# Moving the token operands of an encoder layer's matmuls by 64 to 192 bytes within SBUF

## The chip, the cores and the metric

The kernel runs on one core of a Trainium2 chip. The metric is the device time of one execution in microseconds; times before are the median of three timed runs, and one further execution was recorded by the hardware profiler. The core's engines are TensorE (matmuls, PE in the profile, with its weight loads as PEld), VectorE (DVE), ScalarE (ACT), GpSimd (POOL) and SyncE (SP), which here only issues transfers. SBUF is the memory that matmul operands are read from: 128 partitions, and an address is a byte offset within each of them. PSUM takes the matmuls' results.

## The reference

One layer of an encoder on 512 tokens of width 1024, with 256 memory tokens, all in float32:

```python
n = rms_norm(h, mix_norm_g)
proj = n @ w_in                                  # 1024 x 4608 columns
ya = s5_branch(proj[..., :OFF_U], ...)           # two scans and a GLU
yb = sgu_branch(zu, zv, ...)                     # gating within chunks of 128 tokens
h = h + (gate_a * (ya @ w_proj_a) + gate_b * (yb @ w_proj_b)) @ w_out
h = h + memory_cross_attention(rms_norm(h, g), memn, w_q, w_k, w_v, w_xo)   # 4 heads of 256
h = h + (silu(f @ w_gate) * (f @ w_up)) @ w_down # f = rms_norm(h, ffn_norm_g), width 2816
return rms_norm(h, final_norm_g)
```

`memn` is the normalised memory; keys and values come from it.

## The kernel before

**Split operands.** Every large matrix product is made of three matmuls in a rounded float32 format (`F32R`). Each operand is split into a high part (`hi`, a rounding copy on ScalarE) and a low part (`lo`, the difference, on VectorE; both in `split`, lines 85 and 86). A product is then hi·hi + hi·lo + lo·hi, three matmuls one after the other into one PSUM place (`mm3`, line 314; line 1264 for the FFN).

**Stationary and streamed.** A matmul holds 128 x 128 numbers of one operand in the array and streams the other through it. The stationary operand is loaded by an instruction of its own before each matmul. In `feat` and `product` the weights are stationary and the tokens are streamed, 512 or 256 of them; in `tokm` and the down product the tokens are stationary and 512 columns of weights are streamed. In the profile a matmul is written `out<-streamed,stationary`.

**Order.** A list `plan` has all weight blocks in order of use. Blocks of 512 KB are loaded some places ahead by SyncE's queue, split two ahead, and used. Nothing in this order depends on addresses. The stages are: the input projection with the scan woven in, the gates and merge, `w_out`, then keys (`w_k`, `feat` with 256 tokens), values (`w_v`, `tokm`), queries and attention per head, `w_xo`, the FFN's gate and up products, and the down product.

**The FFN.** The gate and up products use a Winograd-like scheme: a unit (512 columns of `w_gate` or `w_up`) takes seven products `1, 5, 2, 6, 3, 7, 4` of 24 matmuls with 256 tokens each, over sums of weight blocks and sums of token blocks. There are ten units, so 1680 matmuls of 256 columns at line 1264. Products 1, 2, 7 and 4 stream quarters of `fn`, the normalised tokens; products 5, 6 and 3 stream token sums made by `make_op` into tiles `s1`, `s2` and `s4` (`s` in the profile). A remainder of 256 columns is done by `gate_part` (`w_gate`: half of the tokens at a time, so 256 columns, with weights in `s` tiles: `pf<-fn,s`) and by `feat` (`w_up`: 512 columns, `pf<-fn,whi` and `pf<-fn,wlo`).

**Where operands lie.** Weight tiles `whi` and `wlo` take turns in six places whose byte offsets all have the remainder 320 modulo 512. Most token tiles (`xn`, `yb`, `mg`, `hn`, `mn`, the first `qq`) have the same remainder, so their distance from the weights is 0 modulo 512; two small pad tiles (`align`) see to that. Slices within the tiles are multiples of 512 bytes, so one remainder holds for the whole tile. Some tiles stand off on purpose: `token_slot(name, shift)` makes a tile that is 128 elements longer than its content and puts the content `shift` elements (4 bytes each) in; `fn` has shift 16, 64 bytes. `sums_place(i, k, n, shift)` does the same for the `s` tiles: `make_op` uses shift 80, 320 bytes, while weights and the down product's tokens in the same tiles use 0. The keys `kt_hi` and `kt_lo` stand 64 bytes off (tile `shift`). Distances before, streamed minus stationary, modulo 512:

| matmuls | streamed, stationary | columns | distance |
|---|---|---|---|
| most `feat` and `tokm` | tokens and weights, either way | 512 | 0 |
| keys, 192 | `mn`, `whi`/`wlo` | 256 | 0 |
| values, 96 | `whi`/`wlo`, `mn` | 512 | 0 |
| queries of the first head, 96 | `hn`, `whi`/`wlo` | 256 | 0 |
| scores | `kt`, `qq` | 256 | 64 |
| gate remainder, 96 | `fn`, `s` | 256 | 64 |
| up remainder, 48 | `fn`, `whi`/`wlo` | 512 | 64 |
| FFN products 1, 2, 7, 4 | `fn`, `whi`/`wlo` | 256 | 64 |
| FFN products 5, 6, 3 | `s`, `whi`/`wlo` | 256 | 320 |

The tag `mq` of the attention pool has two buffers: first `mn_hi` and `mn_lo`, 8192 bytes a partition each, later `qq` (one head's queries, both parts), the heads in turn.

Of the kernel before, what the change touches and what calls it, by code (L numbers as in the profile page):

```python
# [10 lines left out]
F32R = mybir.dt.float32r  # L11
# [6 lines left out]
P = 128  # L18
D = 1024
T = 512  # L20
NT = T // P
KD = D // P
M = 256
# [29 lines left out]
def hybrid_layer_kernel(  # L53
# [26 lines left out]
    def aux(name, shape=(P, 512)):  # L80
        return pa.tile(list(shape), F32, tag="aux", name=name)

    def split(dst_hi, dst_lo, src, lo_eng=None):

        nc.scalar.copy(dst_hi, src)  # L85
        (lo_eng or nc.vector).tensor_tensor(dst_lo, src, dst_hi.bitcast(F32), ALU.subtract)  # L86
# [23 lines left out]
    def sums_place(i, k, n, shift=0):  # L110
        t = sums_pool[0].tile([P, 2 * k * n + 128], F32R, tag=f"s{i}", name=f"s{i}", bufs=1)
        return t[:, shift:shift + 2 * k * n].rearrange("p (h k n) -> p h k n", h=2, k=k)
# [309 lines left out]
    def gain(src, name):  # L422
        t = np_.tile([P, D], F32, tag="gain", name=name, bufs=2)
        nc.sync.dma_start(t, src.partition_broadcast(P))
        return t
# [52 lines left out]
    def slot(tag, shape, dt, name):  # L478
        return sp.tile(list(shape), dt, tag=tag, name=name)

    def token_slot(name, shift=0):

        t = sp.tile([P, 2 * KD * T + 128], F32R, tag="B", name=name)
        hl = t[:, shift:shift + 2 * KD * T].rearrange("p (h k t) -> p h k t", h=2, k=KD)
        return hl[:, 0], hl[:, 1]
# [557 lines left out]
    ap_ = at.enter_context(tc.tile_pool(name="attn", bufs=1))  # L1043

    h = slot("A", (P, NT, D), F32, "h")
# [2 lines left out]
    hn_hi, hn_lo = token_slot("hn")  # L1048
    hn = (hn_hi, hn_lo)

    mn_hi = ap_.tile([P, KD, M], F32R, tag="mq", name="mn_hi", bufs=2)
    mn_lo = ap_.tile([P, KD, M], F32R, tag="mq", name="mn_lo", bufs=2)
    g_mem = gain(mem_norm_g, "g_mem")

    def mem_norm(t):
# [60 lines left out]

    def q_evac(m, j, ps):
        if j == 0:
            qq = ap_.tile([P, 2, 2, T], F32R, tag="mq", name="qq", bufs=2)
            qs[m // 2] = (qq[:, 0], qq[:, 1])  # L1120
        q_hi, q_lo = qs[m // 2]
        split(q_hi[:, j, :], q_lo[:, j, :], ps)
# [46 lines left out]
    for hd in range(XH):  # L1169
        feat(w_q, hd * XD, hn, KD, q_evac, parts=2 if hd == 0 else 1)  # L1170
        probs = scores(hd)
        if hd > 0:
            values(hd - 1, *pts.pop(0))
        later(1, lambda hd=hd, probs=probs: pts.append(turn_probs(hd, probs)))

    g_f = gain(ffn_norm_g[0], "g_f")
    ot = (ot_hi, ot_lo)
    fn_hi, fn_lo = token_slot("fn", 16)
    fn = (fn_hi, fn_lo)

    tokm(w_xo, 0, ot, KD, add_evac(0, 1, None), hook=lambda: values(XH - 1, *pts.pop()))
# [50 lines left out]
    a11, a12, a21, a22 = full[:, K0, T0], full[:, K1, T0], full[:, K0, T1], full[:, K1, T1]  # L1232

    def make_op(q, i, src):
        hl = sums_place(i, 4, 256, 80)
        ops[q] = (hl[:, 0], hl[:, 1])
        split(*ops[q], src)

    def sum1():
        V.tensor_tensor(a22, a21, a22, ALU.subtract)  # L1240
        make_op(5, 1, a22)

    def sum2():
        V.tensor_tensor(s3, a11, a21, ALU.subtract)
        V.tensor_tensor(a11, a22, a11, ALU.subtract)
        make_op(6, 2, a11)

    def sum4():
        V.tensor_tensor(a12, a12, a11, ALU.add)
        make_op(3, 4, a12)  # L1250
# [232 lines left out]
    for i in range(2):  # L1483
        p = aux("pcut", (P, 256))
# [37 lines left out]
```

## Time and profile before

| | us |
|---|---|
| median of three timed runs (918.16, 923.18, 923.67) | 923.18 |
| profiled execution | 915.85 |
| its span, first to last instruction | 914.1 |
| TensorE busy | 897.4 |
| weight loads busy | 789.2 |
| VectorE busy | 609.0 |
| ScalarE busy | 458.7 |
| mean granted TensorE clock | 0.994 |

The profile's times are of the one profiled execution, in microseconds from its first instruction. A busy TensorE is not one at its peak: matmuls are pipelined, the recorded duration of one is longer than the time until the next one starts, and only runs of many matmuls tell how quickly they follow each other. The chain of work that ended last is followed back from the last instruction; where TensorE never waits, it lists unbroken runs of matmuls with length and count.

### The profile page before, as it was taken

The page shows a single profiled execution, that of the slowest core. Times are in us where ns is not written, and L with a number is a line of the kernel's source. Part 1 is how long each engine was busy: PE and PEld are TensorE (multiplying, and loading weights), DVE is VectorE, ACT ScalarE, POOL GpSimd, SP SyncE. Part 2 cuts the span into 40 slices and gives each one's busy share as a digit, 9 for nine tenths or more (in the row PEclk, how much of TensorE's full clock was granted, in tenths as well). Part 3 has the DMA queues.
Part 4 walks back from the last instruction along what each step waited for, and adds up shares of the span by engine and source line. Part 5 has one row for each costly group of instructions (what it writes and reads, how often), then busy time and mean ns, then how long its engine had stood idle before and what let it go on. Part 6 is the DMA issues. An engine that isn't in the chain of part 4 may idle for free.

```text
span 914.1 us, 14130 instructions
## 1 busy us (share of the span) xinstructions
PE 897.4 (98%) x5510; PEld 789.2 (86%) x5510; DVE 609.0 (67%) x991; ACT 458.7 (50%) x671; POOL 109.1 (12%) x163
## 2 busy tenths in 40 slices
PE   7999999999999999999999999999999999999996
PEld 6888888888888887789998888999999999888875
DVE  5596662888753235868545444786778777899875
ACT  5542995244374333445434433655554555655663
POOL 3003210000025301502000001000000000000000
PEclk8999999999999999999999999999999999999999
DMA  8445263675546655686895217415456463246572
GB/s 269 127 120 151 85 164 126 181 205 133 141 138 158 144 185 156 216 260 191 244 291 147 71 68 233 113 65 142 119 154 144 118 160 94 70 147 207 188 241 82
DMA packets 105987, 142.77 MB, mean 156 GB/s; under 512 B 13232, under 2 KB 73152, under 8 KB 105920
## 3 DMA queue, kind: packets, MB, share of 16 engines
q1 hardware_dynamic: 90688, 120.14, 40.9%
q0 software_dynamic: 12064, 19.37, 12.9%
q10 hardware_dynamic: 3168, 2.36, 0.9%
q8 instruction: 43, 0.70, 0.3%
q14 instruction: 24, 0.20, 0.1%
HBM read 135.06 MB, written 29.85 MB: 180 GB/s over the span
## 4 chain that ended last, share of the span: by engine, by line
PE 86%; ACT 4%; DVE 4%; DMA 3%; issue 2%; POOL 1%; POOLq 0%; SPq 0%; ACTq 0%; DVEq 0%
PE pf L314 31%; PE pt L314 14%; PE px L1264 12%; PE pq L1264 6%; PE dx L314 5%; PE dq L314 3%; PE pv L1264 3%; PE dv L314 2%; PE pk L714 2%; DVE wlo L86 1%; PE ptr L466 1%; PE po L314 1%; PE psc L314 1%; DMA wraw<-dsum 1%; ACT whi L85 1%
## 5 line engine op out<-in xcount | busy, mean ns | idle before, releaser
L86 DVE TENSOR_TENSOR wlo<-wraw,whi 128x1024 fp32r<-128x1024 f32 (+1 forms) x130 | 157.9, 1216 | 130.5 <-ACT whi L85 128.0
L85 ACT CAST whi<-wraw 128x1024 fp32r<-128x1024 f32 x132 | 135.4, 1028 | 174.5 <-PE pf L314 79.7
L314 PE MATMUL pf<-xn,whi 128*128 128x512 f32 x448 | 140.5, 392 | 0.0
L314 PEld LDWEIGHTS pf<-xn,whi 128*128 128x128 f32 x448 | 83.7, 188 | 17.3 <-issue 0.2
L314 PE MATMUL pf<-xn,wlo 128*128 128x512 f32 x224 | 87.6, 391 | 0.0
L1264 PE MATMUL px<-fn,whi 128*128 128x256 f32 x480 | 83.8, 277 | 0.0
L1264 PEld LDWEIGHTS px<-fn,whi 128*128 128x128 f32 x480 | 72.6, 188 | 0.3 <-ACT u L1377 0.2
L85 ACT CAST whi<-b 128x1024 fp32r<-128x1024 f32 x40 | 42.1, 1054 | 55.0 <-PE px L1264 26.8
L86 DVE TENSOR_TENSOR wlo<-b,whi 128x1024 fp32r<-128x1024 f32 x40 | 48.9, 1223 | 28.5 <-ACT whi L85 28.5
L1264 PE MATMUL px<-fn,wlo 128*128 128x256 f32 x240 | 66.3, 276 | 0.0
L314 PE MATMUL dx<-whi,s 128*128 128x512 f32 x170 | 53.9, 391 | 1.4 <-ACT whi L85 1.0
L1264 PE MATMUL pq<-s,whi 128*128 128x256 f32 x320 | 55.0, 276 | 0.0
L314 PEld LDWEIGHTS pf<-xn,wlo 128*128 128x128 f32 x224 | 42.1, 188 | 8.5
L1264 PEld LDWEIGHTS pq<-s,whi 128*128 128x128 f32 x320 | 48.3, 188 | 0.2
L86 DVE TENSOR_TENSOR wlo<-t,whi 128x1024 fp32r<-128x1024 f32 x30 | 36.7, 1224 | 15.9 <-ACT whi L85 15.9
L85 ACT CAST whi<-t 128x1024 fp32r<-128x1024 f32 x30 | 31.6, 1053 | 31.0 <-PE pv L1264 11.3
L314 PE MATMUL pt<-whi,xn 128*128 128x512 f32 x128 | 43.4, 412 | 1.8 <-ACT xn L85 1.5
L1264 PEld LDWEIGHTS px<-fn,wlo 128*128 128x128 f32 x240 | 45.1, 188 | 0.0
L1264 PE MATMUL pq<-s,wlo 128*128 128x256 f32 x160 | 44.2, 276 | 0.0
L314 PE MATMUL pf<-hn,whi 128*128 128x512 f32 (+1 forms) x160 | 41.8, 349 | 0.0
L314 PEld LDWEIGHTS dx<-whi,s 128*128 128x128 f32 x170 | 31.7, 188 | 8.5 <-ACT whi L85 1.2
L314 PE MATMUL dx<-wlo,s 128*128 128x512 f32 x85 | 33.3, 391 | 0.7 <-DVE wlo L86 0.7
(380 smaller groups left out, 2175.3 us busy)
## 6 DMA issues: line engine op xcount, KB each, us to landing
wraw<-in_w_in_dram SPq DMA_DIRECT2D x36, 512.0 KB, 3.8
dsum<-in_w_down_dram SPq DMA_DIRECT2D x20, 512.0 KB, 5.3
wraw<-dsum SPq DMA_DIRECT2D x20, 512.0 KB, 3.6
b<-in_w_gate_dram SPq DMA_DIRECT2D x15, 512.0 KB, 3.6
b<-in_w_up_dram SPq DMA_DIRECT2D x15, 512.0 KB, 3.6
wraw<-in_w_down_dram SPq DMA_DIRECT2D x15, 512.0 KB, 4.1
dsum<-in_w_down_dram POOLq DMA_DIRECT2D x10, 512.0 KB, 7.3
dsum<-dsum POOLq DMA_DIRECT2D x10, 512.0 KB, 6.1
```

What stands on the lines that cost most here:

```text
L85: nc.scalar.copy(dst_hi, src)
L86: (lo_eng or nc.vector).tensor_tensor(dst_lo, src, dst_hi.bitcast(F32), ALU.subtract)
L314: nc.tensor.matmul(ps, a[x], b[y], start=start and i == 0, stop=stop and i == 2, skip_group_check=free)
L466: nc.tensor.transpose(ps[:, j, :], src[:, k * P:(k + 1) * P], ident)
L714: nc.tensor.matmul(ps[32 * j:32 * j + 32, q, :], bd[i][:, g].rearrange("p d c -> p (d c)"), lc(es[i], g), start=(i == 0), stop=False, tile ...
L1264: nc.tensor.matmul(ps[:, j, :], a[x], b[y], start=start and j == k == i == 0, stop=k == 3 and i == 2, skip_group_check=True)
```

## The change

Four places move; no instruction is added, removed or put elsewhere in the order.

```diff
-    mn_hi = ap_.tile([P, KD, M], F32R, tag="mq", name="mn_hi", bufs=2)
-    mn_lo = ap_.tile([P, KD, M], F32R, tag="mq", name="mn_lo", bufs=2)
+    mn_hi, mn_lo = (ap_.tile([P, KD * M + 64], F32R, tag="mq", name=nm, bufs=2)[:, 48:48 + KD * M]
+                    .rearrange("p (k t) -> p k t", k=KD) for nm in ("mn_hi", "mn_lo"))
...
-            qq = ap_.tile([P, 2, 2, T], F32R, tag="mq", name="qq", bufs=2)
+            qq = (ap_.tile([P, KD * M + 64], F32R, tag="mq", name="qq", bufs=2)[:, 0:KD * M]
+                  .rearrange("p (h k t) -> p h k t", h=2, k=2))
...
-    fn_hi, fn_lo = token_slot("fn", 16)
+    fn_hi, fn_lo = token_slot("fn", 32)
...
-        hl = sums_place(i, 4, 256, 80)
+        hl = sums_place(i, 4, 256, 32)
```

The memory tokens `mn` stand 48 elements (192 bytes) in, and the two buffers of `mq` are 256 bytes longer each, so the second buffer starts 256 bytes later and what follows in the pool 512 bytes later. `qq` starts at its buffer's beginning. `fn` stands 32 elements (128 bytes) in instead of 16, the token sums 32 instead of 80. Distances after: FFN products and the gate and up remainders 128; keys 192 (`mn_hi`) and 448 (`mn_lo`); values 320 and 64; scores 64 and, for the heads in the second buffer, 320.

## The prediction

> **What bounds the kernel now.** I read the page first: its span line, its busy line and its slices.
>
> ```profile
> span 914.1 us, 14130 instructions
> ...
> PE 897.4 (98%) x5510; PEld 789.2 (86%) x5510; DVE 609.0 (67%) x991; ACT 458.7 (50%) x671; POOL 109.1 (12%) x163
> ...
> PE   7999999999999999999999999999999999999996
> ...
> PEclk8999999999999999999999999999999999999999
> ```
>
> TensorE is busy from the first slice to the last, and the granted clock is full almost throughout. No instruction comes or goes with the change; it moves addresses. So the question is only how quickly one matmul follows the other, and whether that depends on where its operands lie. A mean duration does not say that, because matmuls are pipelined. The chain that ended last does: it has the length and count of each unbroken run, so length by count is the pace.
>
> ```profile
> 169.55 3.57 PE psv L962 x32
> ...
> 434.45 10.55 PE pf L314 x88
> 445.00 21.79 PE pt L314 x96
> 466.79 11.51 PE pf L314 x96
> ...
> 583.51 2.59 PE pf L314 x22
> ...
> 612.87 2.72 PE pq L1264 x24
> 615.59 8.16 PE px L1264 x72
> ...
> 804.95 2.83 PE pq L1264 x24
> 807.78 6.84 PE dx L314 x30
> 814.62 14.96 PE dq L314 x66
> ```
>
> Columns: start in us, length in us, work, count. Call the distance of the streamed operand from the stationary one, in bytes and modulo 512, d. Runs of 256 columns: keys (434.45) and first queries (466.79), both d = 0, go at 119.9 ns. The FFN products at 612.87 and 615.59 (`s` tokens d = 320, `fn` tokens d = 64) go at 113.3 ns. The same kinds of product go slower elsewhere: 2.59/22 = 117.7 ns for `fn` (583.51), 2.83/24 = 117.9 for `s` (804.95). Starts of single matmuls confirm two levels with little between: of 1680 products about 1560 are 113 or 114 ns apart and 109 are 117 to 120, always whole stretches, and a stretch changes level only after an interruption. So d = 0 has one pace (120.0), and d = 64 and 320 have two, 113.3 and 117.8.
>
> Why can an address matter? The timeline shows it.
>
> ```profile
> 612.93 0.28 PE L1264 MATMUL pq<-s,wlo 128*128 128x256 f32 x1
> 612.93 0.30 PEld L1264 LDWEIGHTS pq<-s,whi 128*128 128x128 f32 x2
> ```
>
> The load of the next weights starts with the matmul, so both read SBUF side by side, and both need nearly the whole interval. The trace does not show how they disturb each other. It shows that the paces are 17 and 18 times 6.667 ns, 34 times for 512 columns (14.96/66 = 226.7), and 53/3 times for the slow level, which looks like whole fetch turns lost. It also bounds the pace from below: `psv` (128 float32 columns, a full load each) goes at 3.57/32 = 111.6 ns.
>
> On this the Trainium skill speaks against the change: "SBUF — State Buffer", section "SBUF: two separate sides", lets only VectorE and GpSimd contend among the engines and gives TensorE a second, independent port for its weights. By it the sum would be zero. The trace disagrees as it stands, with 120.0 against 113.3 ns for one shape at two distances.
>
> **The change part by part.** Remainders follow from the pools: weights `whi` and `wlo` are at 320 modulo 512 everywhere.
>
> 1. `fn` from d = 64 to 128, and tokens of `make_op` from 320 to 128. 1680 products, and 96 half-width gate matmuls (`pf<-fn,s`). What the trace lacks is any run at d = 128. The bounds: 111.6 ns below (`psv`), 120.0 above (the worst row at 256 columns). The nearest rows are 64 and 320; they have equal paces, so I take the period to be 256 bytes. Then d = 128 is the place farthest from 0, where it is worst, and I take 113.3 ns, the better level of its neighbours. On the profiled execution that saves only where it was slow: 109 products x 4.4 = 0.5 us, 96 gate matmuls x 4.4 = 0.4 us. At 111.6 it would be 1776 x 1.7 = 3.0 us more, at 120.0 it would lose 1560 x 6.7 + 205 x 2.2 = 10.9 us.
>
> 2. `mn` from d = 0 to 192; its low half lands at 448, since the tile is 256 bytes longer and the second buffer starts that much later. Both are 192 modulo 256. 192 matmuls now at 120.0; the neighbour rows give 113.3 or 117.8, so 1.3 or 0.4 us; nothing if 192 behaves like 0. I take 1.3.
>
> 3. `mn` is the stationary operand in the value product: 96 matmuls of 512 columns go from d = 0 to 320 (modulo 512), 64 modulo 256. Now 21.79/96 = 227.0. The row at 64 is `pf<-fn` of the remainder's up product, 229 ns from start to start: +0.2 us. The `po` run in the chain (2.31 us for 10) is the far end, 231: +0.4.
>
> 4. The 48 matmuls of 512 columns of that up product go from 64 to 128: between 226.7 and 231, so within 0.1 us either way; zero.
>
> 5. `qq`: its second buffer moves by 256 bytes, so two heads' scores go from d = 64 to 320, two rows with one pace: zero. Everything behind `mq` in its pool moves by 512 bytes and keeps its remainder.
>
> 6. Evictions write the same shapes to other offsets: zero. They lie beside TensorE (DVE 77% busy from 612 to 788 us, ACT 53%), and would need to grow by a quarter before DVE is late next.
>
> All of it is on the path, since TensorE has no gaps there: in the products' window the windows view shows 176.00 of 176.00 us busy.
>
> ```profile
> 612.00:788.00 176.00, 176.00 (x1551) 175.86 (x1550) 135.15 (x135) 92.42 (x112) 10.21 (x8) 1.00 0.49 126
> ```
>
> Columns: stretch, its length, then busy time of PE, PEld, DVE, ACT and POOL, the clock, DMA share and GB/s. Weight traffic is at half of the DMA engines, so a pace some per cent quicker finds its blocks ready.
>
> Sum against the profiled execution (915.85 us: span 914.1 and 1.75 around it): -0.5 - 0.4 - 1.3 + 0.2 = -2.0, so **913.9 us**.
>
> **How that stands to the median.** The timed runs are 918.16, 923.18 and 923.67 us, so the profiled execution is quicker than all of them. The two levels would explain it: had the long stretch run at 117.8, the execution would take 1560 x 4.45 = 6.9 us more, 922.8, which is the upper pair; a flip on the way gives 918. After most interruptions in this trace the level is 117.8, and the long stretch got 113.3 on leaving the 512-column run at 611 us. So I read the median as one of the slow level, and the forecast is 1.0% under it only if d = 128 has no slow level, or is seldom in it. I allow half a microsecond for that and say 914.5.
>
> **Rivals.**
> - Still two levels: d = 128 behaves as 64 does, and timed runs mostly sit at 117.8. For it: nothing shows that the slow level goes away with distance. Against it: d = 0 has a single level, so the number of levels does depend on d. Time 922.8 - 0.4 = 922, or 917 to 919 with a mixture.
> - Slower, the other side: at 128 bytes the load and the stream meet as often as at 0, because the stream advances over the weights' place all the time and the distance only shifts when they meet. Price 120.0 ns a product. It decides from a pace above 117.8, where it passes the median's level. 915.85 + 10.9 = 926.7, or +0.4%. A further lost turn (126.7) would be 1560 x 13.3 + 205 x 8.9 = 22.6 us, 938. For it: 512-column runs have the opposite order (229 at 64, 226.7 at 0), so farther is not always better. Against it: 64 and 320 both reach 113.3.
> - Better than the rows here: 111.6 ns everywhere, 913.9 - 3.0 = 911. For it: `psv` does it, at d = 0. Against it: no 256-column run of this type goes below 113.3.
> - No effect at all: the operands' distance is not what makes 120 of 113, and the keys and the products differ for another reason. Time as before, 916 to 923. Against it: the first queries stream the same whole-token layout as `fn`, with the same weights buffers, and differ in d.
>
> "TensorE: Matmul & The Clock Gate", section "Back-to-back issue gap" of the Trainium skill, counts 262 cycles for 256 columns, 109.2 ns; by it the products would have 1776 x 4.1 = 7.3 us more to win, an estimate of 907 us. The transposes in this trace (4 in 0.44 us) do reach that pace, but not one of its 256-column runs does.
>
> **How the numbers follow.** 113.3 on most timed runs: 0.40, time 914.5. Two levels or a mixture: 0.23, 917 to 923. No effect: 0.04. At 120: 0.15, 926.7. Worse: 0.07. 111.6 or better: 0.11, 911. The range takes in the first five but the worse one: 910.5 to 927.0, which leaves out the worse case and half of the last, 0.13. One per cent, about what a measurement of this kernel can tell from no change, is 914.0 at the lower side of the median. Half of the main case and all of the last lie below it: 0.20 + 0.11 - 0.02 for a run that mixes = 0.29. Slower by over 1% is above 932.4, the worse case: 0.07, and 0.01 for something not thought of: 0.08. The rest, 0.63, lies within.
>
> **What would show it.** In the chain after: px and pq runs of 24 in 2.72 us also near 585 and 805 us (step 1), where they took 2.83; 88 of the keys in about 9.97 us instead of 10.55 (step 2); the value product of 96 in 22.0 instead of 21.79 (step 3). The prediction is wrong if products stay at 2.83 for 24 in the long stretch, or are at 2.88 or above, or if runs under 2.68 appear.

## The result and the profile after

The changed kernel takes 925.5 us (median of 20 executions, 922.75 to 930.17); the kernel before, measured beside it, takes 917.19 us (20 executions, 914.84 to 927.97). The ratio is 1.0066, 95% interval 1.0045 to 1.0087: slower by two thirds of a per cent. (The two medians alone would give 1.009, the means 1.0067: the times of the kernel before fall into two groups, as shown below, and its median lies in the lower one.) The forecast was 914.5 us, so its direction was wrong; 926.7 us was the slower rival.

The page of the changed kernel, span, busy times and slices as before:

```profile
span 923.6 us, 14130 instructions
...
PE 906.7 (98%) x5510; PEld 797.7 (86%) x5510; DVE 608.9 (66%) x991; ACT 458.2 (50%) x671; POOL 108.7 (12%) x163
...
PEclk9999999999999999999999999999999999999999
```

The same 5510 matmuls keep TensorE busy 9.3 us longer, its weight loads 8.5 us, at no lower clock, and the span is 9.5 us longer. The other engines' busy times are the same within half a microsecond. Where the time went is in the chain that ended last (start in us, length in us, work, count):

```profile
426.31 4.78 PE pf L314 x42
...
432.21 10.37 PE pf L314 x88
442.58 22.40 PE pt L314 x96
...
595.48 16.84 PE pf L314 x96
612.32 2.89 PE pq L1265 x24
615.21 8.64 PE px L1265 x72
...
809.62 2.87 PE px L1265 x24
814.76 2.88 PE pq L1265 x24
```

Products that took 2.72 us for 24 take 2.88: 120.0 ns a matmul, what the keys had at distance 0. From the first product 5 to the last (starts 612.32 and 814.76) it is 202.44 us; before, it was 804.95 - 612.87 = 192.08. These 10.4 us are more than the whole loss. By its 20th microsecond, before any moved place is used, this execution was 1.7 us ahead, with more of the clock granted in the first slice (9 tenths instead of 8); that is no part of the change, since `tokens_96` and `before_break` below, whose memory tokens were not moved, were as far ahead. The keys got quicker (42 in 4.78 us and 88 in 10.37 instead of 5.04 and 10.55), the value product slower (96 in 22.40 instead of 21.79), and the run with the up remainder slower (96 in 16.84 instead of 16.65). Of before, two of these lines did not stand above:

```profile
428.30 5.04 PE pf L314 x42
...
596.21 16.65 PE pf L314 x96
```

The groups with shapes kept apart show the same through durations, which are some 163 ns longer than the pace:

```profile
L1265 PE MATMUL px<-fn,whi 128*128 128x256 f32 x480 | 88.1, 283 | 0.0
L1265 PE MATMUL pq<-s,whi 128*128 128x256 f32 x320 | 58.1, 283 | 0.0
L314 PE MATMUL pf<-mn_lo,whi 128*128 128x256 f32 x64 | 18.0, 282 | 0.0
L314 PE MATMUL pt<-whi,mn_lo 128*128 128x512 f32 x32 | 12.7, 397 | 0.0
```

The same groups of before had means of 277, 276, 285 and 389 ns.

### The profile page after: what moved, and what is told of

Read it like the earlier page. It is cut to its first block, busy times and chain, and to the rows that moved or that the text cites. A ratio compares the mean times of both kernels' runs of the same rounds, so it can differ in the third digit from the quotient of the medians.

```text
span 923.6 us, 14130 instructions
## 1 busy us (share of the span) xinstructions
PE 906.7 (98%) x5510; PEld 797.7 (86%) x5510; DVE 608.9 (66%) x991; ACT 458.2 (50%) x671; POOL 108.7 (12%) x163
## 4 chain that ended last, share of the span: by engine, by line
PE 83%; DVE 5%; ACT 4%; DMA 4%; issue 2%; POOL 1%; SPq 0%; POOLq 0%; DVEq 0%; ACTq 0%
PE pf L314 31%; PE px L1265 12%; PE pt L314 11%; PE pq L1265 6%; PE dx L314 5%; PE dq L314 3%; PE pv L1265 3%; DVE wlo L86 2%; PE dv L314 2%; PE pk L714 1%; ACT whi L85 1%; DMA b<-in_w_gate_dram 1%; PE po L314 1%; PE psc L314 1%; DMA wraw<-in_w_in_dram 1%
## 5 line engine op out<-in xcount | busy, mean ns | idle before, releaser
L1265 PE MATMUL px<-fn,whi 128*128 128x256 f32 x480 | 88.1, 283 | 0.0
L1265 PEld LDWEIGHTS px<-fn,whi 128*128 128x128 f32 x480 | 74.8, 189 | 0.3 <-ACT u L1378 0.2
L1265 PE MATMUL px<-fn,wlo 128*128 128x256 f32 x240 | 68.3, 285 | 0.0
L1265 PE MATMUL pq<-s,whi 128*128 128x256 f32 x320 | 58.1, 283 | 0.0
```

The costliest lines, as they stand in the source:

```text
L1265: nc.tensor.matmul(ps[:, j, :], a[x], b[y], start=start and j == k == i == 0, stop=k == 3 and i == 2, skip_group_check=True)
```

## The experiments

**Which half of the change.** First the tokens alone at 128 (memory tokens as before), and the memory tokens alone moved (tokens as before).

```diff
# tokens_only: the kernel before with
-    fn_hi, fn_lo = token_slot("fn", 16)
+    fn_hi, fn_lo = token_slot("fn", 32)
-        hl = sums_place(i, 4, 256, 80)
+        hl = sums_place(i, 4, 256, 32)
# keys_only: the changed kernel with those two lines put back
```

> The kernel before with the tokens at 128 bytes and the memory tokens left where they were. Theory 1: products at 2.88 us for 24, so 10 us longer than an execution of the kernel before that has 2.72, 3 longer than one at 2.83: 926, ratio 1.005 to 1.010. Rival 3 (the moved keys put the products on another level): as the kernel before, 916 to 923.

Measured: 925.63 us (12 executions, 922.85 to 928.93), ratio 1.0064 (1.0032 to 1.0096). The tokens alone are the loss. One detail differs from the changed kernel: the products of this profiled execution go at 118.7 ns, not 120.0.

```profile
616.18 2.85 PE pq L1264 x24
619.03 8.54 PE px L1264 x72
...
816.55 2.88 PE pq L1264 x24
```

So 128 also has two paces that a whole stretch can keep, 118.7 and 120.0 (levels, as the prediction calls them). First to last product 5: 200.37 us, 8.3 more than before, and 1560 x (118.7 - 113.3) = 8.4.

> The changed kernel with the tokens back at 64 and 320 and only the memory tokens moved. Theory 1: 88 keys in 10.0 to 10.4 us instead of 10.55, the value product 96 in 22.4 instead of 21.8, together -0.6 to +0.2 us; products 2.72 or 2.83: 915 to 923, ratio 0.998 to 1.002. Rival 3: 924 to 926, products at 2.88.

Measured: 922.78 us (12 executions, 913.77 to 926.04), ratio 1.0025 (0.9986 to 1.0064): no difference that can be told. In its chain the keys and values are those of the changed kernel, and the products those of the kernel before:

```profile
432.11 10.37 PE pf L314 x88
442.48 22.40 PE pt L314 x96
```

Four of its executions lie below 918 us and eight between 920 and 927. The kernel before, beside it, does the same: of 29 executions 12 are at 913.7 to 918.2, 17 at 921.1 to 927.8, and none between. The granted clock does not tell the groups apart: its mean is 0.9956 in the lower and 0.9952 in the upper. The next experiments are about these two groups too.

**The pace by distance.** A kernel that runs only the products' matmuls, at one distance after the other, in outline:

```diff
+    for d in (0, 16, ..., 240, 320, 384):   # 72 matmuls of 256 columns each
+        four transposes; matmuls with the streamed operand d bytes from the weights
+    the same in reverse order, without the transposes
+    for d in (0, 64, 128): weights and streamed operand both 64 bytes further   # y
+    for d in (0, 16, ..., 240): 48 matmuls of 512 columns                       # w
```

> This kernel leaves out the whole layer: it loads one weight block and some rows of x, splits both, and runs the gate products' matmuls (hi-hi, hi-lo, lo-hi) over and over at one distance after the other, d = 0, 16, ... 240, 320 and 384 bytes; a d16x is 72 matmuls of 256 columns at 16 bytes, first each behind four transposes, then in reverse order with nothing between; a d16w is 48 matmuls of 512 columns; y is 256 columns with weights and tokens both 64 bytes further. Theory 1 (only the distance counts, modulo 128): 120.0 ns a matmul at 0, 128 and 384, 113.3 or 117.8 at 64, 192 and 320, a lower or equal pace somewhere between; y as x. Rival 2 (modulo 256, with 64 and 320 alone good and 192 as bad as 128): 120 at 192. Rival 3 (the level is caught on entry, whatever the distance): in the reverse order one level is carried from block to block, and the two orders differ. Where weights' own remainder counted, y would differ from x.

In the trace the transposes of 0 to 112 in the first pass run ahead of all these blocks, so that these eight follow each other without transposes in both passes. The chain names the distance:

```profile
46.81 8.48 PE d64x L72 x72
...
72.57 8.17 PE d112x L72 x72
...
117.05 8.18 PE d192x L72 x72
...
246.40 8.54 PE d128x L72 x72
...
314.34 8.64 PE d0x L72 x72
...
332.48 8.17 PE d64y L72 x72
341.08 8.54 PE d128y L72 x72
350.06 10.91 PE d0w L72 x48
...
488.93 11.21 PE d192w L72 x48
```

Mean interval between starts in the settled second half of each block, in ns:

```
distance       0    16    32    48    64    80    96   112   128   144   160   176   192   208   224   240
256, first   120.0 118.7 116.7 118.4 117.8 120.0 120.0 113.3 118.7 118.6 117.3 119.3 113.3 118.9 118.4 117.2
256, reverse 120.0 116.7 117.8 118.3 117.8 120.0 120.0 113.3 118.7 118.7 118.7 119.3 113.3 119.3 118.3 117.2
512          226.7 231.7 233.4 233.3 228.9 231.1 233.3 231.1 232.2 233.3 234.2 233.3 233.3 234.7 233.3 236.7
```

At 320 the pace is that of 64 and at 384 that of 128 (117.8 and 118.7), so a period of 256 bytes fits here for 256 columns, as I had assumed; theory 1's period of 128 falls, since 192 is not as 64 and 128 not as 0. The y blocks, after settling, have 120.0 at 0 and 118.7 at 128 as the x blocks do, although the streamed operand then lies where it lies in the x blocks of 64 and 192: so it is not the streamed operand's own place that counts. At 64, however, y has 113.3 and x 117.8 in both orders. The kernels show both at this distance; that the weights' own remainder has no part in which of them comes is not shown. Rival 2 falls at 192; rival 3 falls because both orders give nearly the same row, although in the second the pace changes from block to block with nothing between. What also falls is any smooth curve: 112 is at 113.3, its neighbours 96 and 128 at 120.0 and 118.7.

**192 and 96 in the kernel.**

```diff
# tokens_192: shifts 48 and 48 (elements of 4 bytes); tokens_96: 24 and 24
```

> The kernel before with fn and the token sums at 192 bytes. Theory 1: as at 64, products at 2.72 or 2.83 us for 24, 915 to 923. Rival 2: 2.88, 926.

Measured: 917.15 us (12 executions, 915.41 to 921.43), ratio 0.9971 (0.9940 to 1.0001). Products at 113.3 ns, and only one execution above 920 us.

```profile
616.26 8.16 PE px L1264 x72
```

> Tokens at 96 bytes, 16 from the place before. By the benchmarks 120.0 ns at every entry: 2.88 us for 24, 925 to 927 in every execution, ratio 1.005 to 1.010. By the prediction's rule (better the farther from 0, up to 128) 2.72, 915.

Measured: 927.78 us (9 executions, 925.30 to 931.56), ratio 1.0097 (1.0062 to 1.0132).

```profile
615.80 2.88 PE pq L1264 x24
618.68 8.64 PE px L1264 x72
```

The benchmark's 120.0 carries over, and the prediction's rule (better the farther from 0, up to 128) is refuted on both sides of 112.

**What picks a level.** Eight entries for each of nine distances, behind one to four transposes or one to four matmuls of 512 columns, and blocks with half the weights' columns (h), in outline:

```diff
+    for d in (0, 32, 64, 96, 112, 128, 160, 192, 224):
+        for each of 8 entries: 48 matmuls of 256 columns
+    for d in (0, 64, 128, 192): the same with 64 columns of weights, two entries
```

> The layer is left out again. For each of nine distances, eight blocks of 48 matmuls of 256 columns, entered in eight ways: behind one to four transposes, and behind one to four matmuls of 512 columns at distance 0. Theory 4 (each distance has its own few levels, and what runs just before picks one): at 0 only 120.0; at 64 both 113.3 and 117.8; at 128 118.7 and 120.0 but never 113.3; at 192 and 112 mostly 113.3. Rival 5 (any level at any distance, the first benchmark's order made the difference): 113.3 at 128 or 120.0 at 192 in some of the eight. The blocks named h have 64 columns of weights instead of 128, so a load half as long: if the lost turns come from the load and the stream meeting, their paces at 0 and 128 fall by several ns towards 109; if the stream's own addresses were the cause, they stay at 120 and 118.7.

Settled intervals in ns (at 0 the operands came late, so the eight blocks ran into one):

```
  0   120.0                                     112   113.3 in all eight
 32   116.5 to 116.8                            128   118.7 seven times, 120.0 once
 64   117.8 in all eight                        160   117.3 three times, 118.7 five
 96   120.0 in all eight                        192   113.3 four times, 117.8 four
224   118.3 or 118.4 in all eight
64 columns of weights:   0: 120.0, 113.3   64: 116.7   128: 116.6   192: 119.0
```

Each distance has one or two levels of its own. 128 never shows 113.3, 192 never 120.0; so rival 5 falls. Theory 4 missed at 64: it expected both levels, and the x blocks of the three benchmarks have 117.8 there at all 14 entries. 113.3 at 64 was seen only in the kernels and in the y block, whose weights lie 64 bytes further than those of the x blocks. 112 is the one distance here with 113.3 at every entry. The half loads miss what was expected of both sides: the paces do change with the number of the weights' columns, but not towards 109, and at 192 they get slower. Fewer columns of weights also mean that fewer partitions of PSUM are written, so that the load is what takes part remains likely and not shown.

> The kernel before with four transposes more ahead of the ten units. Theory 4: the long stretch is entered as the other stretches in the trace are, behind transposes, and goes at 117.8: 2.83 us for 24, so 0.5 for the transposes and 7 us more than an execution with 2.72: all of its executions about 923, with none near 915. Rival 5, or levels that are no property of the entry: two groups as in the kernel before, 915 and 922.

```diff
     V.tensor_tensor(pair[:, 0, T1], pair[:, 0, T1], pair[:, 1, T1], ALU.subtract)
+    brk = aux("brk", (P, 4, P))
+    for j in range(4):
+        nc.tensor.transpose(brk[:, j, :], ident, ident)
```

Measured: 922.05 us (12 executions, 915.35 to 926.35), ratio 0.9999 (0.9964 to 1.0034); four executions below 919 and eight above 921; beside it the kernel before has 13 and 16. So the expectation of one group at 923 failed: four transposes do not settle the level. But the profiled execution, the one of 926.35 us, shows the slow level through the whole stretch:

```profile
616.15 0.44 PE brk L1313 x4
616.59 2.83 PE pq L1264 x24
619.42 5.65 PE px L1264 x48
```

Its last product 5 starts at 815.53: 198.94 us from first to last, 6.9 more than the 192.08 of the kernel before. No execution of the upper group was profiled without the four transposes, so this is the nearest view of that group.

> The same four transposes in the kernel with tokens at 192 bytes. Theory 4: stays at 113.3, 2.72 us for 24, 0.5 us over the kernel with tokens at 192: 917. If 192 only has its level from the entry, 923.

Measured: 916.73 us (12 executions, 914.57 to 919.91), ratio 0.9959 (0.9930 to 0.9988), none above 920; 113.3 ns throughout the stretch.

**Versions that could beat both kernels.** The first has tokens at 192 and the keys' places for the scores at 192; the other two have tokens at 112, the last of them the memory tokens too.

```diff
# tokens_scores_192: shifts 48 and 48, and
-    shift = ap_.tile([P, 16], F32, name="shift")
+    shift = ap_.tile([P, 48], F32, name="shift")
# tokens_112: the same with shifts 28 and 28; all_112: also mn in [:, 28:28 + KD * M]
```

> Tokens at 192 bytes and the keys' places for the scores too (from 64 to 192 behind the queries). Theory 4: products at 2.72, score runs at 113.3 instead of 117.8, which is 96 matmuls and 0.4 us: 915 to 917 in nearly all executions, ratio to the kernel before 0.995 to 0.999, whichever share of that one's executions are at 922.

Measured: 915.91 us (12 executions, 914.52 to 923.12), ratio 0.9960 (0.9929 to 0.9990). The scores did not follow: their runs stay at 2.12 us for 18, 117.8 ns, the other level of 192, so that part of the expectation failed. So this is the kernel with tokens at 192 in all that counts.

> Tokens at 112 bytes, scores' keys at 192. By the benchmarks (113.3 in every entry at 112) the products are at 2.72 us for 24 in every execution: 915 to 917, ratio to the kernel before 0.995 to 0.998, and no execution near 922. If the benchmark does not carry over, levels between 116 and 120 appear: 920 to 926.

Measured: 916.92 us (12 executions, 914.90 to 918.24), ratio 0.9975 (0.9948 to 1.0002); 9 of 28 executions of the kernel before beside it are above 920, none of these. (In this batch the two groups are less clean: three executions of the kernel before lie between 918.4 and 920.1.)

> The same, and the memory tokens at 112 too: keys at 113.3 instead of 120 in their longer stretches (-1.0 us), the value product at the 233.3 that 512 columns have at 144 instead of 226.9 (+0.6 us): 0.4 us less than with the memory tokens at 0, which is too little to be told in the times; in the chain 88 keys in 9.97 instead of 10.55 us and 96 value matmuls in 22.4 instead of 21.8.

Measured: 915.58 us (12 executions, 913.73 to 919.65), ratio 0.9974 (0.9947 to 1.0002). The chain has the two expected pieces:

```profile
433.71 10.01 PE pf L314 x88
443.72 22.43 PE pt L314 x96
```

None of these versions is shown to be quicker than the lower group of the kernel before, which lies at about 916 us as they do. What they change is the share of executions above 920 us: with tokens at 192, 2 of 36 (33 of 58 of the kernel before beside them), with tokens at 112 none of 24 (9 of 28). Only with 192 does the interval lie wholly under 1, in two of three versions.

**Is it the load at all?** Loads of 128, 64 and 32 columns beside the same stream of 256, four entries each, in outline:

```diff
+    for d in (0, 64, 112, 128, 192):
+        for m in (128, 64, 32): four entries, 48 matmuls with m columns of weights
```

> The layer is left out. 256 columns streamed at five distances with 128 columns of weights (x), 64 (h) and 32 (q), four entries each: behind one and four transposes, and behind two and three matmuls of 512 columns. Theory 6 (a meeting of load and stream costs a turn, and a load of 32 columns reads so little that hardly any is left): q at about 109 ns at every distance, h between q and x or on other levels of its own, x as in the second benchmark (112: 113.3 in all four). Rival 7 (what costs turns is the stream beside any load, however short, or the change from one matmul to the next): q stays at 113 or above, and differs by distance as x does.

```
columns        0             64                          112                         128                         192
128        120.0         117.8 all                   113.3 all                   118.7 all                   113.3 117.8 113.3 117.8
 64        113.3 all     116.7 116.7 116.7 113.3     116.7 115.5 120.0 116.7     116.7 116.6 120.0 116.6     119.0 all
 32        117.8 117.8 113.3 117.8   113.3 120.0 116.7 113.3   113.3 all   113.3 115.6 113.3 113.3   113.3 116.7 113.3 113.3
```

At 0 the four blocks of 128 columns ran into one. A quarter of the load leaves 113.3 as the commonest pace and never gives 109. Theory 6 falls as it was stated. Rival 7 has the floor right, but not the differences: which distance is slow depends on the number of the weights' columns. Each of the three benchmarks is one execution; where they share distances with 128 columns of weights (0, 64, 112, 128 and 192), they show the same levels.

## Why the prediction was wrong

**The step that failed is step 1.** "Then d = 128 is the place farthest from 0, where it is worst, and I take 113.3 ns": the period of 256 bytes held, the rule did not. The pace is no smooth function of the distance, and 128 showed the levels 118.7 and 120.0 and no other. With 120.0 for the 1560 products of the long stretch the step's own price, 1560 x 6.7 = 10.4 us, is what the stretch lost from first to last product 5. A rule drawn from two measured points (0, and 64 with 320) had been stretched to a third where the trace had no run.

**The rival that came true** was "Slower, the other side", with its price of 120.0 ns and its 926.7 us (925.5 measured, 925.38 profiled); the price was right, 10.4 us in the stretch against 10.9. Its reason, load and stream meeting as often as at 0, is not shown. The warning beside it was sound: 512 columns have an order of their own (226.7 at 0, 228.9 at 64, 231 to 237 at most other distances).

**Steps 2 and 3, the memory tokens.** Their price was mis-sized. Keys at 192 take both levels here, 113.8 ns in the run of 42 and 117.8 in the run of 88; the mean interval, interruptions left out, fell from 119.7 to 116.0 over some 185 matmuls: -0.7 us and not -1.3. The value product went to 233.3 ns a matmul and not 229: +0.6 us and not +0.2. The benchmark has 228.9 for 512 columns at 64, which is what the up remainder had before, so here the distance modulo 256 does not tell the pace; 512 columns at 320, where one half of this product stands, were not run. Together the two steps come to nothing, as the kernel with the memory tokens alone moved shows. Step 4 cost nearly 0.2 us instead of nothing, by the run of 96 that holds the up remainder. Steps 5 and 6 show nothing in the chain.

**How the forecast stood to the median.** The two groups of the kernel before are real, and they are about as far apart as was computed: 6.9 us in the stretch of the one profile that caught the slow level, of the kernel with four transposes more. That the upper group is this level in the kernel before itself is likely, and not shown. But I read the median of three as the kernel's usual time. Of 20 executions 12 are in the lower group, and the median is 917.19. So what could be won by staying at 113.3 was at most the slow group's share.

**The other rivals.** "Two levels" at 64's values and "no effect" are refuted by 118.7 and 120.0 at 128. "Better than the rows", 111.6 ns, was seen nowhere: 113.3 is the lowest settled pace in three benchmarks. The two quicker rows that the prediction had, `psv` and the transposes, are of 128 columns, so they say little of 256. The 262 cycles, 109.2 ns, that the section "Back-to-back issue gap" of the Trainium skill's "TensorE: Matmul & The Clock Gate" gives for an isolated matmul of 256 columns are not reached at any distance or load tried. The section "SBUF: two separate sides" of the Trainium skill's "SBUF — State Buffer", which gives TensorE a second independent read port for its weights, does not foresee what was measured: 113.3 to 120.0 ns with nothing but the distance between the two operands changed.

**What stays open.** Whether requests of the load and the stream meet, which ones, and why 112 is good and 96 and 128 are not. What picks the level where there are two: transposes ahead of the stretch did not. Why fewer columns of weights make some distances slower. Whether the weights' own remainder decides between 113.3 and 117.8 at 64, and why the value product is at 233.3.

## What to carry to other kernels

Where 128 columns of weights are loaded beside a stream of 256, as here, the distance of the two operands within SBUF is worth some 6% of the matmul pace (113.3 to 120.0 ns), and it can't be interpolated: measure it in a small kernel at every distance of a period, with several entries, before a choice is put into the large one. Judge a distance by its worst level, not by the one that a profile happened to catch; here 64 and 192 have both 113.3 and 117.8, 112 only 113.3 in the benchmarks. And look at the spread of the times before trusting a median of three: two groups 7 us apart were visible in it.

## What the runs showed of the hardware

- Many settled paces are whole thirds of 6.667 ns: 113.3, 117.8 and 120.0 are 51, 53 and 54 of them for three matmuls, 226.7, 228.9, 231.1 and 233.3 are 102, 103, 104 and 105. The others settle between, 116.7 and 118.7 among them.
- One stretch keeps its level over 177 to 187 us and 1560 matmuls until something interrupts it. The same program has two groups of times, about 916 and 923 us, as far apart as two such levels make it.
- For 512 columns distance 0 is the best of sixteen (226.7 ns; the worst 236.7 at 240); for 256 columns it is among the worst (120.0, as at 80 and 96).
- A load of 32 columns of weights, a quarter of the full one, does not make the 256-column stream quicker than 113.3 ns.
